# Token differences from raw tokens, unsplit in DRAM; four gate buffers; output weights split during the branch projections

## The chip, the core and the metric

The kernel runs on one core of one Trainium2 chip. The metric is the device time of one execution in microseconds, told as the median of several runs. The engines are TensorE (PE), VectorE (DVE), ScalarE (ACT), GpSimd (POOL) and SyncE (SP), whose queue issues most of the DMAs.

## The reference

One encoder block over 1024 tokens of width 1024, in float32. After an RMS norm, one input projection feeds three mixers and their gates, and a merge follows:

```python
h = rms_norm(x, g_pre)
a_qkv, bq, bk, bv, mq, ga, gb, gm, mg = split(h @ w_in)
oa = dilated_window_attention(rope(a_qkv), windows (128,1), (512,4), (2048,16)), merged by softmax of log-denominators
ob = grouped_query_attention(qk-norm, axial rope)          # 8 heads, 2 kv heads
om = cross_attention(mq, rms_norm(mem) @ w_mem_kv)         # 256 memory rows
ya, yb, ym = (oa * silu(ga)) @ w_br_a, (ob * silu(gb)) @ w_br_b, (om * silu(gm)) @ w_br_m
gates = sigmoid(mg + b_merge)                              # three times 1024 wide
merged = gates[0] * ya + gates[1] * yb + gates[2] * ym
out = x + rms_norm(merged @ w_out, g_post)
```

## The kernel before

**Split operands.** A float32 operand is held as two parts of a shorter format, a high part (a copy made by ACT) and a low part (the operand less the high part, made by DVE); the helper `split` issues these two. A product is then three matmuls: high by high, low by high, high by low. `hh[k]` and `hl[k]` are the two parts of the transposed tokens, scaled by `g_pre`, for the eight blocks of 128 channels; a tile is 128 x 1024.

**Stages, in order of time** (us from the start of the profiled span): start and memory branch (0 to 223), branch B with its attention (223 to 488), branch A (488 to 1050), the merge gates in pairs (1050 to 1272), the branch projections (1272 to 1413, called Y below), the output projection (1413 to the end). PE's order is written out by hand throughout: a weave interleaves attention pieces with dense units by their costs. In the pairs and in Y the orders of ACT, DVE, POOL and SP are the order of the code as well; in the branches a scheduler sets them, and `issue_after` holds a piece behind a named instruction.

**Gate pairs.** 22 of the 24 units of the gate projection are done two at a time, 11 pairs, by a Strassen-Winograd scheme with 7 products of half size in place of 8. A pair `n` runs through slots `i` = 0 to 6; in each, PE does one product of 12 matmuls (`prod`), DVE and ACT evacuate the product before (`evac`), and `slot` issues preparations: weight sums on POOL (`weight_sum`), their splits (`block_of`, `own_blocks`), weight loads (`load_pair`). The product order of all pairs but the last is A11, A12, S2, S3, S4, S1, A22, with the token operands B11, B21, T2, T3, B22, T1, T4. `gate_out` forms one gate half: an addition and a product on DVE into a buffer `rs`, then a tanh on ACT and a store to `thd` from ACT's queue. A pair stores four.

**Token differences.** T1 to T4 are differences of token blocks. They are made once, in branch B, by `token_block(k)` for four `k`: the sums `hh + hl` restore a block, DVE subtracts, `split` makes the two parts, and SP stores both to `tsd`. One of these steps is taken after a score maximum (`row_max`, L715) at positions 0, 1 and 3 of eight, as long as any are left. Before the last item of branch A, T2 and T3 are loaded (`load_block`); at the start of the pairs T1 and T4, between the weight loads of pair 1. T4 goes to `hh[0..3]` and `hl[0..3]`.

**Y.** 24 steps `m` (branch `n`, output block `f`), 24 matmuls each. In step `m`, after its matmuls are queued: evacuation of step `m - 1` (DVE multiplies by the gate `th`, POOL adds to `accs[f]`), loads for step `m + 2` (weights `wr`, gate `th` from `thd`), in some steps loads of a mixer output `ot` and its gate path `gt` and of `raw` reciprocals, their product and split into `hh`, `hl`, the weight split of step `m + 1`, and from step 15 on the loads of `w_out` into `raw`, split from step 16 on into `wo`.

**Output.** For each of eight token tiles, eight pieces of `accs` are split to an operand, then 48 matmuls, a norm, the residual and the store.

Of the kernel before, what the change touches and what calls it, by code (L numbers as in the profile page):

```python
# [14 lines left out]
D = 1024  # L15
# [35 lines left out]
def block(ctx: ExitStack, tc: tile.TileContext, x, xT, memT, cst, msk, bcst, tabA, gpost,  # L51
# [179 lines left out]
    wgd = dram.tile([4, 2, 3, S], F32, name="wgd")  # L231
    tsd = dram.tile([4, 4, P, 2, 512], F32, name="tsd")

# [410 lines left out]
    with tc.tile_pool(name="ba", bufs=1, reuse_waits="tile") as ba:  # L644
# [34 lines left out]
        def token_block(k):  # L679

            tb = [ba.tile([P, 512], F32, name=f"tb{j}", bufs=1) for j in range(4)]

            def whole(dst, i, e):
                return lambda: V.tensor_tensor(dst, hh[i][:, half[e]].bitcast(F32), hl[i][:, half[e]].bitcast(F32), op=OP.add)

            def sub(dst, x, y):
                return lambda: V.tensor_tensor(dst, x, y, op=OP.subtract)

            def store(j, src):
                def fn():  # L690
                    h = ba.tile([P, 512], R, name="tbh", bufs=2)
                    l = ba.tile([P, 512], R, name="tbl", bufs=2)
                    split(h, l, src)
                    for x, part in enumerate((h, l)):
                        nc.sync.dma_start(tsd[j, k, :, x], part.bitcast(F32))
                return fn

            b11, b12, b22, b21 = tb
            return [whole(b12, k, 1), whole(b11, k, 0), sub(b11, b12, b11), store(0, b11),
                    whole(b22, k + 4, 1), sub(b12, b22, b12), store(2, b12),  # L700
                    sub(b22, b22, b11), store(1, b22), whole(b21, k + 4, 0), sub(b21, b21, b22), store(3, b21)]

        def b_att():
# [69 lines left out]
            for n in range(128 + LAG_F + 8):  # L773
                if n < 128:
                    i, x = divmod(n, 8)
                    row_max(i, x)
                    if n % 32 == 0:
                        blocks += token_block(n // 32)
                    if blocks and x in (0, 1, 3):
                        with tc.issue_after(fp["last"].ins):  # L780
                            blocks.pop(0)()
                    yield 216
                    if i % 2 and i < 15 and x == 4:
                        q_prep((i + 1) // 2)
                        yield 436
                else:
                    yield END_PAD
                if n % 8 == LAG_S % 8 and 0 <= n - LAG_S < 128:
                    shift((n - LAG_S) // 8)
                    yield 109  # L790
                m = n - LAG_T
                if m < 0:
                    yield START_PAD
                elif m < 128:
                    scores(*divmod(m, 8))
                    yield 432
                m = n - LAG_P
                if 0 <= m < 128 and m % 8 == 7:
                    pv(m // 8)
                    yield 8 * 432  # L800
                m = n - LAG_F
                if m >= 0 and m % 8 == 7 and m < 128:
                    final(m // 8)
                    yield 432
# [27 lines left out]
    with tc.tile_pool(name="aa", bufs=1, reuse_waits="tile") as aa:  # L832
# [237 lines left out]
        def plan(it, pre, nxt):  # L1070
# [3 lines left out]
            def combining(T):  # L1074
                if todo and T == STEP_T[-len(todo)]:
                    with tc.issue_after(fp["last"].ins):
                        todo.pop(0)()

            def ready():
                if pre and pre["key"][1] == 2:  # L1080
# [4 lines left out]
            for T in range(NT if it else 4):  # L1085
# [4 lines left out]
                if it:  # L1090
                    out.append(it["soft"][T])
                out.append((lambda T=T: combining(T), 0.0))
                if T < 2:
                    if pre:
# [87 lines left out]

        TB, WHOLE = {}, {}

        def token_tiles(nm, tiles):
            for t in tiles:
                k = len(TB.setdefault(nm, []))
                WHOLE[nm, k] = t
                TB[nm].append([t[:, half[x]] for x in range(2)])

        def load_block(nm, ks=None):
            for k in ks or range(len(TB[nm])):
                src = tsd[int(nm[1]) - 1, k]
                if (nm, k) in WHOLE:
                    nc.sync.dma_start(WHOLE[nm, k].bitcast(F32), src.rearrange("p x t -> p (x t)"))
                else:
                    for x in range(2):
                        nc.sync.dma_start(TB[nm][k][x].bitcast(F32), src[:, x])

# [7 lines left out]
        for n in range(len(seq)):  # L1207
# [7 lines left out]
            if last:  # L1215
# [5 lines left out]
                load_block("T2")  # L1221
                load_block("T3")
            pieces = plan(items[n], items[n - 1] if n else None, items[n + 1])
            if last:
# [13 lines left out]
    SF = [sr.tile([P, 512], F32, name=f"sf{j}") for j in range(4)]  # L1238
    token_tiles("T1", [ab.tile([P, S], R, name=f"a{c}", bufs=2) for c in "qk"])
    token_tiles("T1", [t1l.tile([P, S], R, name=f"T1{k}") for k in (2, 3)])  # L1240
# [38 lines left out]
    def gate_out(n, u, t, x, z):  # L1279
        r = sr.tile([P, 512], F32, name="rs", bufs=2)  # L1280
        j = pairs[n][u]
# [27 lines left out]
    def g_load(i, k):  # L1309
        ot = pre["p"].tile([P, S], F32, name="ot", bufs=4)  # L1310
        nc.sync.dma_start(ot, od[i, k])
        gt = pre["p"].tile([P, S], F32, name="gt", bufs=2)
        nc.sync.dma_start(gt, g2d[i, k])
        GG[i, k] = [ot, gt]

    def r_load(k):
        rt = my.tile([P, S], F32, name="raw", bufs=2)
        for h in range(2):
# [32 lines left out]
    def slot(n, i):  # L1351
# [7 lines left out]
        for nm in todo_[i] if i < len(todo_) else ():  # L1359
            block_of(n, nm)  # L1360
        if n < last:
            if i == 3:
# [35 lines left out]
    load_pair(1, 0)  # L1398
    load_block("T1", (0, 1))
    load_pair(1, 1)  # L1400
    load_block("T1", (2, 3))
    load_block("T4")
    before = None
    for n in range(len(pairs)):
# [23 lines left out]
    def th_load(m):  # L1428
        if m < len(steps):
            _, i, f = steps[m]  # L1430
            THS[m] = my.tile([P, S], F32, name="th", bufs=3)
            nc.sync.dma_start(THS[m], thd[8 * i + f])

    def wo_load(k):
        raws[k] = my.tile([P, D], F32, name="raw", bufs=2)
        nc.sync.dma_start(raws[k], wout[k])
# [13 lines left out]
    def y_evac(m, s):  # L1450
# [6 lines left out]
        else:  # L1457
            V.scalar_tensor_tensor(th, th, 1.0, sv, op0=OP.add, op1=OP.mult)  # L1458
            G.tensor_tensor(accs[f], accs[f], th, op=OP.add)  # L1459

    th_load(0)
    th_load(1)
    yp = None
    for m, (n, i, f) in enumerate(steps):
# [14 lines left out]
        if n < 2:  # L1479
            if f - 1 in (0, 1, 3, 5):  # L1480
                g_mult(j, f // 2)
            if f - 2 in (0, 1, 3, 5):
                g_split(j, (f - 1) // 2, slice(0, S))
        if m >= 15 and m < 23:
            wo_load(m - 15)
        if n == 2:
            split(*wo[f], raws[f])
    y_evac(*yp)
    manual.__exit__(None, None, None)

# [5 lines left out]
    for T in range(NT):  # L1496
        t = slice(T * 128, T * 128 + 128)
        ah = wp.tile([P, 8, 128], R, name="wh")
        al = wp.tile([P, 8, 128], R, name="wl")
        for k in range(8):  # L1500
            A.activation(ah[:, k], accs[k][:, t], AF.Copy, scale=0.5)
            V.scalar_tensor_tensor(al[:, k], accs[k][:, t], 0.5, ah[:, k].bitcast(F32), op0=OP.mult, op1=OP.subtract)
        sv = pss().rearrange("p a b -> p (a b)")
# [163 lines left out]
```

## Time and profile before

| | |
|---|---|
| median of 3 runs | 1517.31 us (1515.16 to 1519.26) |
| the profiled execution's own time | 1514.58 us |
| its span in the profile | 1512.8 us |
| mean granted TensorE clock | 0.993 |
| busy share of the span: PE, DVE, ACT, POOL | 97%, 64%, 41%, 35% |
| DMA | 151.26 MB, mean 100 GB/s |

The page of the profile gives busy time per engine; the views of the trace give stretches, groups of instructions, and waits. A wait line names the waiting engine and line, and what ended the wait. Matmuls are pipelined: one is shown 0.39 us long while the next starts sooner, so a busy PE is not a PE at its pace. Each row of stretches has, per engine, busy time and the number of instructions.

### The profile page before, as it was taken

What the parts mean: (1) busy time and instruction counts of PE and PEld (TensorE: products, weight loads), DVE (VectorE), ACT (ScalarE), POOL (GpSimd) and SP (SyncE); (2) the same over time, 40 slices, a digit from 0 to 9 for tenths busy, and PEclk for the clock granted to TensorE, in tenths of its full rate; (3) what the DMA queues carried; (4) which work ended last, traced back from release to release, by engine and by line L of the source; (5) the groups of instructions that cost most, each with busy time, mean ns of one, the idle gap of its engine ahead of it and who ended that gap; (6) DMA issues with size and microseconds to landing.
All of it is one profiled execution on the core that took longest, in us unless ns stands there. A gap on an engine that the chain in (4) does not pass through costs nothing.

```text
span 1512.8 us, 20951 instructions
## 1 busy us (share of the span) xinstructions
PE 1463.6 (97%) x7712; PEld 1161.6 (77%) x7712; DVE 972.2 (64%) x1701; ACT 617.4 (41%) x1396; POOL 523.1 (35%) x401
## 2 busy tenths in 40 slices
PE   8999988999999999999999999999999999999998
PEld 7899965556556888888888888888788777787787
DVE  7755569888874566556656856653677677565543
ACT  6534444555555145344443444344333333122321
POOL 1426314656657232123223312311344221034422
PEclk9999999999999999999999999999999999999999
DMA  6322022122121210112112111343543444856332
GB/s 241 100 97 70 29 64 79 63 75 66 66 79 58 88 42 29 43 44 72 56 43 73 44 42 49 104 137 108 187 133 121 150 163 160 253 211 234 114 110 97
DMA packets 69014, 151.26 MB, mean 100 GB/s; under 512 B 15344, under 2 KB 25264, under 8 KB 68784
## 3 DMA queue, kind: packets, MB, share of 16 engines
q1 hardware_dynamic: 62432, 138.27, 27.6%
q10 hardware_dynamic: 6480, 11.67, 2.1%
q8 instruction: 60, 0.98, 0.3%
q14 instruction: 42, 0.34, 0.1%
HBM read 111.79 MB, written 38.11 MB: 99 GB/s over the span
## 4 chain that ended last, share of the span: by engine, by line
PE 64%; DVE 13%; issue 9%; DMA 5%; ACT 4%; POOL 4%; SPq 0%; ACTq 0%; DVEq 0%; POOLq 0%
PE d L143 12%; PE d L147 12%; PE d L145 12%; PE sc L1518 4%; PE s L125 4%; PE ov L748 3%; PE tr L1015 3%; PE s L952 2%; DVE bn L715 2%; DMA thd<-rs 2%; DMA raw<-in_wout 2%; PE d L534 2%; DVE og L1151 1%; DVE rs L1283 1%; PE s L733 1%
## 5 line engine op out<-in xcount | busy, mean ns | idle before, releaser
L143 PE MATMUL d<-hh,wh 128*128 128x512 f32 x864 | 346.0, 400 | 3.9 <-DVE fth L222 3.9
L147 PE MATMUL d<-hh,wl 128*128 128x512 f32 x864 | 347.0, 402 | 0.0
L145 PE MATMUL d<-hl,wh 128*128 128x512 f32 x864 | 342.4, 396 | 0.0
L143 PEld LDWEIGHTS d<-hh,wh 128*128 128x128 f32 x864 | 162.9, 189 | 45.3 <-issue 7.7
L147 PEld LDWEIGHTS d<-hh,wl 128*128 128x128 f32 x864 | 162.9, 188 | 36.0 <-issue 5.2
L145 PEld LDWEIGHTS d<-hl,wh 128*128 128x128 f32 x864 | 162.9, 189 | 34.8 <-issue 4.7
L105 ACT ACTIVATE wh<-wr 128x1024 fp32r<-128x1024 f32 (+1 forms) x89 | 83.6, 942 | 232.8 <-PE d L145 155.3
L739 POOL TENSOR_TENSOR bl<-bl,bp 128x512 f32<-128x512 f32 x96 | 137.7, 1435 | 67.7 <-ACT bp L735 62.4
L125 PE MATMUL sc<-hh,wh 128*128 128x512 f32 x384 | 120.9, 395 | 7.1 <-ACT wh L105 2.7
L871 POOL TENSOR_TENSOR aq<-t1a,t2a 128x512 f32<-128x512 f32 x24 | 54.6, 2274 | 163.5 <-DVE t1a L865 163.5
L865 DVE SCALAR_TENSOR_TENSOR t2a<-d,tab 32x512 f32<-32x512 f32 x96 | 65.9, 687 | 62.8 <-PE d L147 57.8
L106 DVE TENSOR_TENSOR wl<-wr,wh 128x1024 fp32r<-128x1024 f32 x65 | 87.4, 1346 | 29.1 <-ACT wh L105 29.1
L735 ACT ACTIVATE bp<-s 128x512 f32<-128x512 f32 x128 | 75.1, 594 | 50.8 <-PE s L733 50.0
L871 POOL TENSOR_TENSOR ak<-t1a,t2a 128x512 f32<-128x512 f32 x24 | 55.1, 2296 | 117.5 <-DVE t1a L864 117.5
L715 DVE TENSOR_REDUCE bn<-tr 128x1 f32<-128x512 f32 x128 | 85.6, 682 | 13.7 <-PE tr L714 13.0
L125 PEld LDWEIGHTS sc<-hh,wh 128*128 128x128 f32 x384 | 72.4, 190 | 25.5 <-DVE wh L106 4.6
L1459 POOL TENSOR_TENSOR acc<-acc,th 128x1024 f32<-128x1024 f32 x16 | 45.6, 2848 | 125.4 <-DVE th L1458 125.4
L1254 POOL TENSOR_TENSOR sf<-wr 128x512 f32<-128x512 f32 x22 | 28.8, 1331 | 154.0 <-DVE ch L106 101.2
L864 DVE TENSOR_TENSOR t2a<-d,tab 32x512 f32<-32x512 f32 x96 | 66.0, 687 | 24.9 <-PE d L147 21.2
L964 DVE CUSTOM_DVE_ANT_0 pra<-s,mask 128x192 f32<-128x192 f32 (+2 forms) x192 | 56.7, 348 | 33.9 <-PE s L952 23.8
L125 PE MATMUL sc<-hl,wh 128*128 128x512 f32 x192 | 75.6, 394 | 1.2 <-DVE hl L106 1.2
L1001 ACT ACTIVATE app<-tr 128x384 f32<-128x384 f32 (+2 forms) x96 | 45.9, 478 | 71.6 <-PE tr L998 46.2
(299 smaller groups left out, 3160.7 us busy)
## 6 DMA issues: line engine op xcount, KB each, us to landing
wr<-in_wu SPq DMA_DIRECT2D x76, 512.0 KB
th<-thd SPq DMA_DIRECT2D x24, 512.0 KB
thd<-rs ACTq DMA_DIRECT2D x44, 256.0 KB
g2d<-fth SPq DMA_DIRECT2D x24, 256.0 KB
wgt<-wgd SPq DMA_DIRECT2D x24, 256.0 KB
ot<-od SPq DMA_DIRECT2D x12, 512.0 KB
gt<-g2d SPq DMA_DIRECT2D x12, 512.0 KB
wr<-in_wbr SPq DMA_DIRECT2D x24, 256.0 KB
```

Of the source, the lines that this page charges most:

```text
L105: A.activation(dst_h, src, AF.Copy)
L106: V.tensor_tensor(dst_l, src, dst_h.bitcast(F32), op=OP.subtract)
L125: PE.matmul(out_ps, a, b, start=i == 0, stop=i == n - 1)
L143: PE.matmul(dst, wh[:, k, :], hh[k][:, t], start=k == 0, stop=False)
L145: PE.matmul(dst, wh[:, k, :], hl[k][:, t], start=False, stop=False)
L147: PE.matmul(dst, wl[:, k, :], hh[k][:, t], start=False, stop=k == 7)
L715: fp["last"] = V.tensor_reduce(st[i]["n"][:, j, c:c + 1], s, axis=AX.X, op=OP.min)
L735: A.activation(pp, s, AF.Exp, scale=-1.0)
L739: G.tensor_tensor(lsum[i % 2], lsum[i % 2], pp, op=OP.add)
L864: return V.tensor_tensor(out, x, y, op=OP.mult)
L865: return V.scalar_tensor_tensor(out, x, scale, y, op0=OP.mult, op1=OP.mult)
L871: G.tensor_tensor(half_of(o, half, g), classes(t1, g), classes(t2, g), op=OP.add)
```

## The change

Token differences are made from the raw tokens: `token_block` loads two tiles of `xT`, scales them by `g_pre` on ACT in place, subtracts on DVE and stores each difference once, unsplit. `tsd` is half as large. T2, T3 and the first half of T1 are loaded before or in the last item of branch A, the rest of T1 and T4 at the start of the pairs, all into the low tile; `split_block` splits in place on use: T2 and T3 in the last item of A, T1 and T4 in slots 2 to 5 of pair 0. `rs` gets four buffers, `th` four, `raw` three, `gt` one and, for some, a `raw` buffer. `w_out` is loaded in steps 10 to 17 and split in steps 12 to 19. The first output operand is split in step 23 and behind the last evacuation, and the last accumulation is done on DVE.

```diff
-    tsd = dram.tile([4, 4, P, 2, 512], F32, name="tsd")
+    tsd = dram.tile([4, 4, P, 512], F32, name="tsd")
...
         def token_block(k):
-            tb = [ba.tile([P, 512], F32, name=f"tb{j}", bufs=1) for j in range(4)]
-            def whole(dst, i, e):
-                return lambda: V.tensor_tensor(dst, hh[i][:, half[e]].bitcast(F32), hl[i][:, half[e]].bitcast(F32), op=OP.add)
-            def sub(dst, x, y):
-                return lambda: V.tensor_tensor(dst, x, y, op=OP.subtract)
-            def store(j, src):
+            x1, x2 = [ba.tile([P, S], F32, name=f"tx{j}", bufs=1) for j in range(2)]
+            for j, t in enumerate((x1, x2)):
+                nc.sync.dma_start(t, xT[k + 4 * j])
+                A.activation(t, t, AF.Copy, scale=cs[:, C_GP + k + 4 * j:C_GP + k + 4 * j + 1])
+            (b11, b12), (b21, b22) = [[t[:, h] for h in half] for t in (x1, x2)]
+            T = [ba.tile([P, 512], F32, name=f"tb{j}", bufs=1) for j in range(4)]
+            def sub(j, x, y):
                 def fn():
-                    h = ba.tile([P, 512], R, name="tbh", bufs=2)
-                    l = ba.tile([P, 512], R, name="tbl", bufs=2)
-                    split(h, l, src)
-                    for x, part in enumerate((h, l)):
-                        nc.sync.dma_start(tsd[j, k, :, x], part.bitcast(F32))
+                    V.tensor_tensor(T[j], x, y, op=OP.subtract)
+                    nc.sync.dma_start(tsd[j, k], T[j])
                 return fn
-            b11, b12, b22, b21 = tb
-            return [whole(b12, k, 1), whole(b11, k, 0), sub(b11, b12, b11), store(0, b11),
-                    whole(b22, k + 4, 1), sub(b12, b22, b12), store(2, b12),
-                    sub(b22, b22, b11), store(1, b22), whole(b21, k + 4, 0), sub(b21, b21, b22), store(3, b21)]
+            return [sub(0, b12, b11), sub(2, b22, b12), sub(1, b22, T[0]), sub(3, b21, T[1])]
...
-                    if n % 32 == 0:
-                        blocks += token_block(n // 32)
-                    if blocks and x in (0, 1, 3):
+                    if n in (18, 42, 66, 90):
+                        blocks += token_block((n - 18) // 24)
+                    if blocks and x in (1, 3) and n % 24 != 19:
...
+            def tokens(T):
+                if T >= 2:
+                    for nm, k in late[:2]:
+                        with tc.issue_after(fp["last"].ins):
+                            split_block(nm, k)
+                    del late[:2]
+                if T == 5:
+                    token_tiles("T1", [ab.tile([P, S], R, name=f"a{c}", bufs=2) for c in "qk"])
+                    load_block("T1", (0, 1))
...
+                if it and not nxt:
+                    out.append((lambda T=T: tokens(T), 0.0))
...
-        def load_block(nm, ks=None):
-            for k in ks or range(len(TB[nm])):
-                src = tsd[int(nm[1]) - 1, k]
-                if (nm, k) in WHOLE:
-                    nc.sync.dma_start(WHOLE[nm, k].bitcast(F32), src.rearrange("p x t -> p (x t)"))
-                else:
-                    for x in range(2):
-                        nc.sync.dma_start(TB[nm][k][x].bitcast(F32), src[:, x])
+        def load_block(nm, ks=range(4)):
+            for k in ks:
+                nc.sync.dma_start(TB[nm][k][1].bitcast(F32), tsd[int(nm[1]) - 1, k])
+        def split_block(nm, k):
+            h, l = TB[nm][k]
+            split(h, l, l.bitcast(F32))
+        late = []
...
+                late += [("T2", k) for k in range(4)] + [("T3", k) for k in range(4)]
...
-        r = sr.tile([P, 512], F32, name="rs", bufs=2)
+        r = sr.tile([P, 512], F32, name="rs", bufs=4)
...
-        gt = pre["p"].tile([P, S], F32, name="gt", bufs=2)
+        gt = my.tile([P, S], F32, name="raw", bufs=3) if i < 2 and k % 2 else pre["p"].tile([P, S], F32, name="gt", bufs=1)
...
-        rt = my.tile([P, S], F32, name="raw", bufs=2)
+        rt = my.tile([P, S], F32, name="raw", bufs=3)
...
+        if first:
+            for nm, k in {2: (("T1", 0), ("T1", 1)), 3: (("T1", 2), ("T1", 3)), 4: (("T4", 0), ("T4", 1)),
+                          5: (("T4", 2), ("T4", 3))}.get(i, ()):
+                split_block(nm, k)
...
     load_pair(1, 0)
-    load_block("T1", (0, 1))
-    load_pair(1, 1)
     load_block("T1", (2, 3))
     load_block("T4")
+    load_pair(1, 1)
...
-            THS[m] = my.tile([P, S], F32, name="th", bufs=3)
+            THS[m] = my.tile([P, S], F32, name="th", bufs=4)
...
-        raws[k] = my.tile([P, D], F32, name="raw", bufs=2)
+        raws[k] = my.tile([P, D], F32, name="raw", bufs=3)
...
-            G.tensor_tensor(accs[f], accs[f], th, op=OP.add)
+            (V if m == 23 else G).tensor_tensor(accs[f], accs[f], th, op=OP.add)
+    def out_split(ah, al, T, k):
+        src = accs[k][:, T * 128:T * 128 + 128]
+        A.activation(ah[:, k], src, AF.Copy, scale=0.5)
+        V.scalar_tensor_tensor(al[:, k], src, 0.5, ah[:, k].bitcast(F32), op0=OP.mult, op1=OP.subtract)
+    WO = (4, 5, 6, 7, 0, 1, 2, 3)
...
-        if m >= 15 and m < 23:
-            wo_load(m - 15)
-        if n == 2:
-            split(*wo[f], raws[f])
+        if m >= 10:
+            if m < 18:
+                wo_load(WO[m - 10])
+            if 12 <= m < 20:
+                split(*wo[WO[m - 12]], raws[WO[m - 12]])
+        if m == 23:
+            first = out_operand()
+            for k in range(6):
+                out_split(*first, 0, k)
     y_evac(*yp)
+    for k in (6, 7):
+        out_split(*first, 0, k)
```

## The prediction

> **What bounds the kernel now.** I read the stages first (busy time per stretch: PE, weight loads, DVE, ACT, POOL, then granted clock, DMA share, GB/s), then PE's waits.
>
> ```profile
> core 0: us, PE busy (x) PEld busy (x) DVE busy (x) ACT busy (x) POOL busy (x), PEclk, DMA share, GB/s
> 223.00:488.00 265.00, 252.84 (x1065) 157.94 (x1065) 208.44 (x292) 141.82 (x243) 155.69 (x110) 1.00 0.21 72
> 488.00:1049.90 561.90, 561.50 (x3337) 454.25 (x3335) 332.81 (x752) 227.63 (x680) 155.15 (x95) 1.00 0.20 61
> 1049.90:1271.90 222.00, 215.72 (x926) 174.59 (x924) 160.10 (x203) 84.28 (x128) 68.63 (x42) 0.98 0.46 153
> 1271.90:1413.00 141.10, 132.83 (x568) 107.16 (x569) 84.05 (x81) 32.56 (x43) 38.79 (x14) 0.99 0.68 232
> 1413.00:1512.80 99.80, 91.28 (x418) 75.85 (x416) 45.23 (x84) 23.52 (x85) 29.31 (x24) 0.97 0.25 90
> ```
> ```profile
> engine line waited for: us in total, times, longest us
> PE tr L714 <- DVE bn L715: 8.0, 20, 0.9
> PE s L371 <- ACT hh L272: 5.8, 1, 5.8
> PE tr L596 <- DVE pm L588: 4.2, 2, 2.6
> PE s L125 <- ACT ch L105: 4.1, 3, 2.4
> PE d L143 <- DVE fth L222: 3.9, 2, 2.2
> PE sc L125 <- ACT wh L105: 2.7, 2, 1.6
> PE sc L125 <- DVE wh L106: 2.6, 3, 1.2
> PE sc L1518 <- DVE wl L1502: 2.3, 1, 2.3
> PE sc L125 <- DVE sp L1277: 1.9, 1, 1.9
> PE s L125 <- DMA hh<-tsd: 1.3, 1, 1.3
> PE sc L125 <- DVE hl L106: 1.2, 1, 1.2
> ```
>
> The stretches shown are: branch B, branch A, the gate pairs, the branch projections ("Y"), the output projection. The 223 us before them hold the start and the memory branch, which the change leaves alone. PE is the bound in all of them, so an edit pays only where it removes a PE wait. Branch A has none (561.5 of 561.9 us). The change touches the other waits from B on: L714 and L143 (B), `ch` and `hh<-tsd` (pairs), `sp` (the join), the rows with `sc` (Y and output).
>
> Waits alone understate the loss. The pace of undisturbed matmuls is the distance of their starts:
>
> ```profile
> 1092.32 0.39 PE L125 MATMUL s<-hh,wh 128*128 128x512 f32 x1
> ...
> 1097.53 0.39 PE L125 MATMUL s<-hh,wl 128*128 128x512 f32 x1
> ```
>
> These are the first and last of 24: 5.21 / 23 = 0.2265 us. The pairs have 11 x 7 x 12 = 924 matmuls, 209.3 us at that pace, and took 222.0: 12.7 lost. Y has 24 x 24 = 576, 130.5 us, and took 141.1: 10.6 lost. What a short wait costs is seen around the one for `hh<-tsd`:
>
> ```profile
> 1070.30 0.67 PE L125 MATMUL s<-hl,ch 128*128 128x512 f32 x1 [0.30 <-DMA hl<-tsd]
> ```
> ```profile
> 1068.00:1070.00 2.00, 0.67 (x2) 0.19 (x1) 1.65 (x3) 1.00 (x2) 0.00 (x0) 1.00 0.90 275
> 1070.00:1072.00 2.00, 1.70 (x4) 1.00 (x5) 0.00 (x0) 1.07 (x2) 0.00 (x0) 0.62 1.07 255
> 1072.00:1074.00 2.00, 2.00 (x6) 1.56 (x6) 0.00 (x0) 0.00 (x0) 0.00 (x0) 0.53 0.73 279
> ```
>
> Twelve matmuls in 6 us instead of 26.5 is 3.3 us lost for 1.6 us of waiting (1.3 for `hh`, 0.3 for `hl`), because the granted clock fell to 0.53. The Trainium skill (TensorE: Matmul & The Clock Gate, Part 1: The HAM clock gate) states that the clock halves after an idle window of about 3.4 us; by that rule gaps of 1 to 2 us cost only themselves, and the sum below would be some 5 us smaller. The trace shows the halving after 1.6 us, so I keep the surcharge.
>
> **Branch B: token differences from raw tokens.**
>
> ```profile
> L684 DVE TENSOR_TENSOR tb<-hh,hl x16: 671/1170/1509, 225.2 to 456.0; 128x512 f32<-128x512 f32 x16
> L687 DVE TENSOR_TENSOR tb<-tb,tb x16: 670/1064/1781, 228.8 to 458.1; 128x512 f32<-128x512 f32 x16
> L105 ACT ACTIVATE tbh<-tb x16: 613/630/632, 229.5 to 459.3; 128x512 fp32r<-128x512 f32 x16
> L106 DVE TENSOR_TENSOR tbl<-tb,tbh x16: 678/1036/1806, 233.4 to 461.3; 128x512 fp32r<-128x512 f32 x16
> ```
> ```profile
> L105 ACT ACTIVATE wh<-wr 128x1024 fp32r<-128x1024 f32 x65 | 68.7, 1058 | 161.7 <-PE d L145 155.3 <-ACT rs L1284 3.6 <-DMA wr<-in_wu 1.4
> ```
> ```profile
> 255.37 0.50 PE L143 MATMUL d<-hh,wh 128*128 128x512 f32 x1 [2.17 <-DVE fth L222]
> ```
>
> Before: 48 DVE operations at medians of 1.17, 1.06 and 1.04 us, 52 us. After: the 16 subtractions, 17 us. DVE loses 35 of its 208 us. ACT drops 16 x 0.63 = 10.1 and gains 8 scalings of 128x1024 at 1.06 = 8.5. SP drops 32 stores of 256 KB and gains 8 loads of 512 KB and 16 stores: the same bytes in a stretch with DMA share 0.21, so nothing. L714's PE waits are for the row minima `bn`, which stand in DVE's queue behind these operations; the new code places them two steps apart instead of back to back. Two thirds of the operations go, so of the 8.0 us, plus 20 x 0.17 (a matmul is shown 0.39 long at a pace of 0.2265, which hides 0.17 of each gap), plus the L143 wait of 2.2, whose DVE row came late for the same reason, two thirds would be 9. I take **6**, since minima still queue behind other evacuations; bounds 2 and 10, and below nothing by a rival.
>
> **End of branch A.** Eight splits (ACT 0.63, DVE about 0.7 to 1.1 each: 5 and 6 to 9 us) come into its last item. DVE works 333 of 562 us there and ACT 228, and PE has dense work beside it: **0**. Without that cover it would be up to 9.
>
> **Pair 0.** The late transfers were the last of 5.1 MB queued at its start; now 2.5 MB stand there, unsplit, so `hh<-tsd` lands in time. In exchange eight more splits lie in slots 2 to 5, behind in-order work:
>
> ```profile
> 1063.57 0.63 ACT L105 ACTIVATE ch<-sf 128x512 fp32r<-128x512 f32 x1 [3.70 <-POOL sf L1254]
> ```
>
> That is pair 1's S3 block, waiting for POOL's weight sum. T4's first two splits stand behind it on ACT, the other two behind the S2 block after it. From 1063.6 I count ACT done with the last at about 1067 and DVE (S3, T4, T4, evacuation, S2, T4, T4 at 0.7 to 1.1) at about 1069.6. The product A22 starts at 1049.9 + 6 x 2.72 = 1066.2 and wants its third low part at 1067.8, ready at 1069: a wait of 1.2 with some surcharge, 2 to 3 instead of 3.3. I take **1**, bounds -3 and 3. The next late thing is POOL's sums. (`load_pair(1, 1)` moves behind T4's loads but still has under 2.5 MB ahead, against 2 MB before.)
>
> **Four gate buffers.**
>
> ```profile
> DVE rs L1277 <- DMA thd<-rs: 28.3, 11, 6.4
> ```
>
> Once per pair the third gate of the burst S1, S1, A22 waits for the first one's store, up to 6.4 us. Behind it stand on DVE all evacuations and splits, on ACT the tanh and the next `ch` split, for which PE then waits (the 2.4 in `ch` is this one). With four buffers no gate waits for a store of its own burst. Of the 12.7 us lost in the pairs, 3.3 are T4's; the other 9 are mostly these `ch` waits (4.1 plus surcharge) and pieces I can't name. I take **5**, bounds 3 and 7. At the join, the first Y product waits 1.9 for `sp`, the second 1.6 for ACT's `wh` behind the last tanh, both behind such a store; 3.5 and a surcharge of about one. I take **4**, bounds 1 and 5.
>
> **Y: th with four buffers, output weights earlier.**
>
> ```profile
> SPq L1432 <- POOL acc L1459: 60.4, 13, 7.2
> ```
> ```profile
> L1459 POOL TENSOR_TENSOR acc<-acc,th 128x1024 f32<-128x1024 f32 x16 | 45.6, 2848 | 125.4 <-DVE th L1458 125.4
> ```
> ```profile
> L106 DVE TENSOR_TENSOR wh<-wr,wh 128x512 fp32r<-128x512 f32 x24 | 16.4, 684 | 1.8 <-ACT wh L105 1.8
> L1458 DVE SCALAR_TENSOR_TENSOR th<-th,sc 128x1024 f32<-128x1024 f32 x16 | 19.4, 1213 | 2.8 <-PE sc L125 2.8
> ```
> ```profile
> 1345.55 3.42 DVE L106 TENSOR_TENSOR hl<-ot,hh 128x1024 fp32r<-128x1024 f32 x1
> ```
> ```profile
> L106 DVE TENSOR_TENSOR hl<-raw,hh x4: 1226/1226/2059, 1378.3 to 1394.4; 128x1024 fp32r<-128x1024 f32 x4
> ```
>
> SP's queue stands for `th` slots, and every later load with it; a fourth buffer lets each go one step (5.44 us) earlier. The waits `wh L106` (2.6) and `hl L106` (1.2) follow late loads, so with surcharge about 5 of the 10.6 lost in Y hang on this (the rest is the join). Against it: six weight loads (3 MB) move into steps 10 to 15, which makes 13 MB in 43.5 us for steps 8 to 15, 299 GB/s, where the stretch averaged 232 at share 0.68, so about 340 when full. It fits, narrowly. At steps 13 and 14 the weight load's slot is freed only by that same step's split, so SP, and the next `wr` and `th` behind it, stand some 3 us. DVE gains a split in steps 12 to 15: evacuation 1.2, `wh` 0.7, `hl` up to 3.4, weight split 1.2, 6.5 against 5.44 in two of four steps; the lag of 2 us is inside the 3.5 that the next `wh` has. I take **3.5**, bounds -2 and 6.
>
> **Output.** Six of eight first operand tiles move ahead of the last Y unit's end, and the last accumulation goes from POOL (2.8) to DVE (about 1.2). The wait of 2.3 for `wl L1502` with a surcharge of 1.5 goes. I take **3**, bounds 1 and 4.
>
> The Trainium skill (GPSIMD Engine Reference, Specifications) says that DVE instructions with two SBUF inputs contend with GpSimd; the rows 3.42 against 1.23 agree, and by it the moved splits are the last rival here.
>
> **Sum**: 6 + 0 + 1 + 5 + 4 + 3.5 + 3 = 22.5. The profiled execution took 1514.6 (its span 1512.8 and 1.8 around it), so 1492 for such a one; the median of the three runs lies 2.7 higher, 1517.3, so **1495**. The terms' bounds give 7 to 35 off.
>
> **Rivals.**
> *Half comes back.* B's minima queue behind other DVE work and pair 0's splits make PE wait as long as the transfers did: B 2, pair 0 -2, the join 2, Y 1, the rest as above: 11 off, 1506. For it: DVE is 72% busy in the pairs (160.1 of 222). Against: 28 us of that stretch was DVE waiting.
>
> *Slower: ACT behind the raw tokens.* The eight scalings wait in ACT's strict order for their loads. A 512 KB load took
>
> ```profile
> 1383.95 5.10 DMA raw<-in_wout
> ```
>
> and PE has two score banks at about 1.9 us a score (128 in the 238 us to the last `tbl` at 461.3), so ACT may stand some 2.5 us before PE stands. Where a scaling sits right behind its load's issue, PE stops 2.6 us, with the surcharge (3.3 for 1.6) 5.4. Eight of these are 43 us at most, 21 without surcharge; with B's 6 gone, 16.5 remain off and 21 to 43 come on: 1522 to 1544, say 1523. It decides once loads land over 2.5 us after the scaling's turn. Against: the load is issued seven score steps ahead of the first subtraction, and ACT has 123 us free in B.
>
> *Contention in Y.* Weight splits fall beside POOL's sum and take 3.42 like `hl`: steps 12 to 15 then hold 30.6 us of DVE against 21.8, a lag of 8.8 less 3.5, so PE loses 5 and a surcharge of 2, and Y's 3.5 go: 1506. Against: the sum covers 2.8 of each 5.44 us, so rarely two splits.
>
> **How the numbers follow.** Forecast 0.58, half back 0.18, contention 0.09, slower 0.15. A measurement tells 0.3% (4.6 us) from no change. Slower takes that rival's 0.15 less 0.02 for a mild form: 0.13; that and the low ends of the two 1506 cases give 0.07 for the same; faster 0.80. The predicted time is the forecast's own. The range goes from 1484 (terms near their good bounds) to 1515 (the bad bounds and part of the slower case).
>
> **What would show it.** In the profile after: L714's waits under 4 us; no `rs <- thd<-rs` wait; no `hh<-tsd` wait but perhaps one for T4's split; the `sp` and `L1502` waits gone; SP's `th` wait far under 60. Wrong would be ACT waits for `tx` loads in B with PE's score matmuls behind them, or new PE waits for `hl`, `wh` in steps 12 to 17.

## The result, and the profile after

The median of four runs after the change is 1484.65 us (1480.33 to 1485.02), against 1518.28 us (1515.16 to 1520.06) for the kernel before beside it: a ratio of 0.9774, 95% interval 0.9749 to 0.9799. The kernel is faster by 33.6 us. The prediction said 1495, so its sign held and its size was 11 us short; by the ratio (0.9774 x 1517.31 = 1483.0) the time lies 1 us below the low end of its range. The profiled execution took 1480.33 us, its span 1478.5.

The busy time per stretch of the kernel after, cut at the same events as before (branch B, branch A, pairs, Y, output):

```profile
core 0: us, PE busy (x) PEld busy (x) DVE busy (x) ACT busy (x) POOL busy (x), PEclk, DMA share, GB/s
223.00:471.90 248.90, 245.85 (x1061) 159.58 (x1061) 172.83 (x260) 141.71 (x235) 148.59 (x110) 1.00 0.23 76
471.90:1034.30 562.40, 561.82 (x3338) 454.60 (x3337) 337.75 (x760) 232.04 (x688) 155.38 (x95) 1.00 0.20 58
1034.30:1245.40 211.10, 209.85 (x928) 173.47 (x925) 170.11 (x215) 89.44 (x138) 68.71 (x42) 1.00 0.44 146
1245.40:1384.50 139.10, 133.30 (x577) 108.68 (x576) 103.78 (x84) 33.16 (x48) 41.15 (x15) 0.99 0.73 242
1384.50:1478.50 94.00, 87.78 (x410) 73.50 (x409) 40.16 (x76) 21.06 (x77) 22.49 (x22) 0.98 0.26 90
```

Most of the gain lies in two stretches, B and the pairs. To compare kernels I cut each trace at PE events (first row-maximum matmul of B, start of B's last block of 16 value products, first A score, first pair product, first Y product, first output product). In the two profiled executions this gives, in us:

| | B | A | pairs and join | Y | output |
|---|---|---|---|---|---|
| before | 263.78 | 517.21 | 223.80 | 141.16 | 97.92 |
| after | 248.27 | 517.53 | 211.12 | 139.29 | 93.73 |
| gain | 15.5 | -0.3 | 12.7 | 1.9 | 4.2 |

With 0.4 in the start these sum to 34.3 us of span. The 44.9 us between B's last block of value products and A's first score did not change.

The waits of PE after, the groups that answer to those shown of before:

```profile
PE sc L125 <- DVE wh L106: 3.4, 2, 2.2
PE sc L125 <- ACT wh L105: 2.2, 2, 1.9
PE d L143 <- DVE fth L222: 1.7, 1, 1.7
PE tr L707 <- DVE bn L708: 1.3, 3, 0.5
...
PE s L125 <- DVE hl L106: 1.3, 1, 1.3
```

L707 is before's L714: its 20 waits for a row minimum (`row_max` takes it of negated scores) have become 3. The waits for `ch`, for `sp`, for the transfers from `tsd` and for the output's first low part have no row any more. What is left of the pairs is a single wait, for a split of T4 in pair 0, and 5.6 us of the waits from B on lie in Y, in the two `sc` rows. DVE's row of waits for the store of a gate (28.3 us before) is gone as well.

### The profile page after: what moved, and what is told of

Its sections match the earlier page's. It is cut to its first block, busy times and chain, and to the rows that moved or that the text cites. A ratio compares the mean times of both kernels' runs of the same rounds, so it can differ in the third digit from the quotient of the medians.

```text
span 1478.5 us, 20900 instructions
## 1 busy us (share of the span) xinstructions
PE 1446.5 (98%) x7712; PEld 1160.2 (78%) x7712; DVE 966.6 (65%) x1686; ACT 625.3 (42%) x1404; POOL 511.8 (35%) x400
## 3 DMA queue, kind: packets, MB, share of 16 engines
q1 hardware_dynamic: 60272, 134.07, 28.3%
## 4 chain that ended last, share of the span: by engine, by line
PE 83%; DVE 6%; ACT 3%; POOL 2%; DMA 2%; issue 2%; SPq 0%; POOLq 0%; DVEq 0%; ACTq 0%
PE s L125 14%; PE d L143 12%; PE d L147 12%; PE d L145 12%; PE sc L125 8%; PE sc L1538 5%; PE ov L741 3%; PE tr L1008 3%; PE s L945 2%; PE d L534 2%; PE s L726 1%; PE s L725 1%; PE tr L707 1%; DMA th<-thd 1%; PE tr L991 1%
## 5 line engine op out<-in xcount | busy, mean ns | idle before, releaser
L143 PE MATMUL d<-hh,wh 128*128 128x512 f32 x864 | 345.8, 400 | 1.9 <-DVE fth L222 1.7
L143 PEld LDWEIGHTS d<-hh,wh 128*128 128x128 f32 x864 | 162.9, 189 | 43.4 <-issue 7.7
L732 POOL TENSOR_TENSOR bl<-bl,bp 128x512 f32<-128x512 f32 x96 | 130.8, 1362 | 60.8 <-ACT bp L728 55.3
L1465 POOL TENSOR_TENSOR acc<-acc,th 128x1024 f32<-128x1024 f32 x15 | 41.2, 2743 | 120.5 <-DVE th L1464 120.5
L965 ACT ACTIVATE pra<-pra,sts 128x128 f32<-128x128 f32 (+2 forms) x152 | 66.5, 439 | 20.0 <-DVE sts L957 20.0
```

Of the source, the lines that this page charges most:

```text
L143: PE.matmul(dst, wh[:, k, :], hh[k][:, t], start=k == 0, stop=False)
L732: G.tensor_tensor(lsum[i % 2], lsum[i % 2], pp, op=OP.add)
L965: A.activation(src, raw, AF.Exp, scale=-1.0, bias=bias, accum_out=sts[:, h, 1, T:T + 1])
```

## The experiments

"B" below is the first column of the table; each kernel differs from the one after by the edit shown, unless it is said to start from the one before.

### Branch B: how many operations, and where

Theory: DVE's queue ahead of the row minima is the cost, through the number of operations. Rival: their places decide.

```diff
+                    V.tensor_tensor(T[j], x, y, op=OP.subtract)
+                    V.tensor_tensor(T[j], x, y, op=OP.subtract)
                     V.tensor_tensor(T[j], x, y, op=OP.subtract)
```

> The changed kernel with each token subtraction in branch B done three times (48 DVE operations as before, in the 16 places of the change; the result is the same). Theory N (the number of DVE operations ahead of the row minima cost the 15.5 us in B): B, from its first row maximum to its last value product, goes back from 248 to about 260 us or more, the time to about 1497. Theory P (the place: back to back at positions 0 and 1, the burst at B's start, DVE standing for ACT's high part): B stays within 248 to 252, the time within 3 us of 1484.

The median was 1498.12 us (1493.73 to 1500.27), ratio to before 0.9865 (0.9838 to 0.9892). B took 265.09, all of its gain given back. The run is not clean, though: its waits of PE and, in B, of ACT show two causes.

```profile
PE s L727 <- ACT bp L730: 7.0, 5, 2.3
...
PE tr L709 <- DVE bn L710: 4.9, 9, 1.1
```
```profile
ACT tx L684 <- DMA tx<-in_xT: 12.9, 6, 4.5
```

The waits for the minima came back in part, but ACT also stood 12.9 us for raw tokens (4.5 of them at the first load, much as after), and PE 7.0 us for ACT's exponentials. The two belong together: each of these five PE waits ends 1.7 to 1.8 us after the start of a scaling that stood for its load. The first pair, from the timelines of ACT and PE:

```profile
291.47 1.15 ACT L684 ACTIVATE tx<-tx,cs 128x1024 f32<-128x1024 f32 x1 [1.37 <-DMA tx<-in_xT]
```
```profile
293.16 0.50 PE L727 MATMUL s<-QH,KS 128*128 128x512 f32 x1 [2.27 <-ACT bp L730]
```

That is the mechanism of the "slower" rival, at work once the scaling's turn comes 1.4 to 1.8 us ahead of its data. To leave it out, the same 48 operations were given places of their own (`again` is the subtraction without its store):

```diff
-            return [sub(0, b12, b11), sub(2, b22, b12), sub(1, b22, T[0]), sub(3, b21, T[1])]
+            out = []
+            for j, x, y in ((0, b12, b11), (2, b22, b12), (1, b22, T[0]), (3, b21, T[1])):
+                out += [again(j, x, y), again(j, x, y), sub(j, x, y)]
+            return out
...
-                    if blocks and x in (1, 3) and n % 24 != 19:
+                    if blocks and x in (1, 3, 4, 5, 6, 7) and not 19 <= n % 24:
```

> The changed kernel with three subtractions in place of each one in branch B, as before 48, but each in a place of its own (positions 1, 3, 4, 5, 6, 7 of eight). Theory N (number): B at 258 us or more, PE waits for the row maxima 6 us or more. Theory P (bursts: three in a row, or two back to back): B at 253 or less. Theory A (the last kernel with 48 lost time to ACT standing for raw token loads, 12.9 us, not to DVE): B long only if ACT again waits over 8 us for them.

One run, 1489.38 us; B took 257.71, 9.4 more than after and just under theory N's 258. The same stretch, of the spread kernel and then of the one after, and PE's waits of the spread kernel for the minima:

```profile
225.00:475.00 250.00, 240.78 (x1030) 152.79 (x1030) 204.48 (x289) 135.84 (x225) 147.66 (x106) 1.00 0.23 74
```
```profile
225.00:475.00 250.00, 247.63 (x1071) 159.60 (x1071) 171.00 (x255) 140.25 (x231) 151.53 (x112) 1.00 0.23 76
```
```profile
PE tr L721 <- DVE bn L714: 6.5, 6, 2.0
PE tr L713 <- DVE bn L714: 1.9, 5, 0.5
```

The second of these waits is that of the row maxima: 1.9 us, where theory N asked for 6. The first, L721, belongs to another product, the transposition of an item's gathered minima in `shift`, which had no wait before (its line there is L722):

```profile
L722 PE MATMUL tr<-cs,bnm 128*68 128x128 f32 x16 | 4.3, 271 | 0.0
```

Summed over the distances of matmul starts, 7.7 of the 9.4 us arose at these 16 products and 1.2 at the 128 row maxima, where the kernel before had its loss. So 33.5 us more of DVE work cost 9.4 us, 0.3 per operation, but the run does not separate number from place: its operations at positions 3 to 7 are one step apart too, and they moved PE's wait to another product.

Next the opposite: the 16 operations stay and their places move together.

```diff
-                    if blocks and x in (1, 3) and n % 24 != 19:
+                    if blocks and x in (1, 2) and n % 24 != 18:
```

> The changed kernel with its 16 subtractions at positions 1 and 2 of eight, one score step apart, in place of 1 and 3. Theory P: the back to back places cost, B goes from 248.3 to 251 or more, the PE waits for the row maxima from 1.3 to 3 or more. Theory N: B within 0.7 us of 248.3.

One run, 1483.7 us. B took 252.15: 3.9 us more for neighbouring places alone, as theory P has it. PE's wait for the minima went from 1.3 to 2.9.

```profile
PE tr L707 <- DVE bn L708: 2.9, 5, 0.9
```

Last, on the kernel before, the differences from raw tokens with the split and the two stores of before: 32 DVE operations (16 differences, 16 low parts), one at each of the old places 0, 1 and 3. A block's loads start at the row maxima where the change has them.

```diff
-            return [whole(b12, k, 1), whole(b11, k, 0), sub(b11, b12, b11), store(0, b11), ...
+            return [sub(b11, b12, b11), store(0, b11), sub(b12, b22, b12), store(2, b12),
+                    sub(b22, b22, b11), store(1, b22), sub(b21, b21, b22), store(3, b21)]
```

> The kernel before with the differences made from raw tokens but still split and stored as two parts in branch B: 32 DVE operations, 16 of them behind ACT, at positions 0, 1 and 3. Number and place both count by now (48 in places of their own cost 9.4 us more than 16, 16 put one step apart cost 3.9 more). Theory N (number mostly, some 0.3 us for each operation): from the first row maximum to the first score of branch A 300 to 304 us, between 308.7 (48) and 293.2 (16). Theory P (place mostly, since positions 0 and 1 stay): 305 or more.

One run, 1505.29 us; B took 256.32, a gain of 7.5 over before with the 16 sums gone; the 16 low parts, with the other places, make the 8.1 that are left. To A's first score it is 301.2, in theory N's range. PE's wait for the minima stood between the two kernels:

```profile
PE tr L713 <- DVE bn L714: 3.7, 10, 0.8
```

Both theories hold in part. B in order of DVE operations: 48 as before 263.8, 48 spread 257.7, 32 at the old places 256.3, 16 close together 252.2, 16 as in the change 248.3. In each of these kernels PE stands for DVE's queue. How the 15.5 us divide between number and place the runs do not settle: place alone is worth 3.9 us with 16 operations, 48 differ by 6.1 between the old places and the spread ones (where ACT's halves of the splits and the second stores are gone too), and 16 operations fewer at the old places are worth 7.5.

### The pairs: gate buffers against T4's late splits

```diff
-        r = sr.tile([P, 512], F32, name="rs", bufs=4)
+        r = sr.tile([P, 512], F32, name="rs", bufs=2)
```

> The changed kernel with two gate buffers again. Theory G (the gate buffers carry nearly all that the pairs and the join gained): the stretch from the first pair product to the first Y product goes from 211 to 220 to 222 us, the time to about 1494. Rival T (the token transfers carry it): 211 goes to at most 215, the time to at most 1488.

1497.74 us, ratio 0.9863 (0.9837 to 0.9889). Pairs and join took 226.84, 15.7 more than after, 3.0 more than before, and more than theory G's 220 to 222. The waits of PE for the splits of `ch` are back:

```profile
PE s L125 <- ACT ch L105: 5.7, 4, 2.8
...
PE s L125 <- DVE ch L106: 2.4, 2, 2.1
```

And the other way round, four buffers in the kernel before (`raw` and `gt` arranged as after, to have the space):

```diff
-        r = sr.tile([P, 512], F32, name="rs", bufs=2)
+        r = sr.tile([P, 512], F32, name="rs", bufs=4)
```

> The kernel before with four gate buffers, and with gt and raw arranged as in the change so that they fit. Theory G: the stretch from the first pair product to the first Y product goes from 224 to about 214 us, with the wait for the late T4 transfer (3 to 4 us) still there; the time 1507 to 1509. Rival T: 218 or more.

1505.48 us, ratio 0.9919 (0.9894 to 0.9945). Pairs and join took 212.30: the buffers, with the arrangement they need, bring 11.5 of the 12.7 us, and no `ch` row is left. For the transfers of T4, which the change unsplits, 3 to 4 us of waiting were expected; PE waits only this, and 0.4 for `hh`:

```profile
PE s L125 <- DMA hl<-tsd: 1.0, 2, 0.7
```

Unsplit transfers with the splits on use are thus worth 1.2 us beside four buffers (212.30 to 211.12), and cost 3.0 beside two (223.80 to 226.84), each from one profiled execution.

### Y: the fourth gate tile, and the order of SP's queue

```diff
-            THS[m] = my.tile([P, S], F32, name="th", bufs=4)
+            THS[m] = my.tile([P, S], F32, name="th", bufs=3)
```

> The changed kernel with three th buffers. If the fourth buffer is what lets the loads of Y's steps 8 to 16 come in time, as forecast: the PE waits for hl and wh near step 16 (2.2 us before) come back and Y goes from 139.3 to 142 or more. If it does nothing there: Y within 0.7 us of 139.3.

One run, 1486.89 us; Y took 145.08, 5.8 more than after and more than in any other run. Its waits of PE:

```profile
PE sc L125 <- DVE wh L106: 5.1, 5, 2.2
...
PE sc L125 <- ACT wh L105: 2.5, 2, 1.4
```

The waits that before had 96 to 100 us into Y are back (1.42 at 1344.33 and 1.53 at 1346.59), so the fourth tile works as forecast, as far as one run shows. Not all of the 5.8 need be its own: the granted clock over Y was 0.96 in this run and 0.99 after. Yet Y gained only 1.9 in the profiled executions. One of SP's waits around Y's start in the kernel after, then its timeline there, show what came in place of the old waits:

```profile
SPq L1438 <- DMA thd<-rs: 10.0, 1, 10.0
```
```profile
1240.23 10.79 SPq L1438 DMA_DIRECT2D th<-thd  x2
1251.13 0.37 SPq L1342 DMA_DIRECT2D wr<-in_wbr  x1
```

The second `th` load waits until the last gate's store is done, and every later load of Y waits behind it. The stretches (columns as in the table of stretches) show DMA idle, then full, and PE stopped:

```profile
1244.00:1248.00 4.00, 4.00 (x20) 3.30 (x19) 3.10 (x6) 0.72 (x1) 0.00 (x0) 1.00 0.00 1
...
1264.00:1266.00 2.00, 0.89 (x3) 0.46 (x4) 1.69 (x2) 1.04 (x1) 0.00 (x0) 1.00 1.05 418
1270.00:1272.00 2.00, 1.74 (x7) 0.82 (x5) 1.88 (x2) 1.25 (x2) 0.00 (x0) 1.00 1.05 410
1272.00:1274.00 2.00, 0.02 (x1) 0.00 (x0) 2.00 (x3) 1.07 (x2) 0.00 (x0) 1.00 1.01 401
1274.00:1276.00 2.00, 1.73 (x4) 1.45 (x5) 2.00 (x3) 0.00 (x0) 0.00 (x0) 0.50 1.07 365
1276.00:1278.00 2.00, 2.00 (x7) 1.52 (x7) 1.93 (x3) 0.00 (x0) 0.00 (x0) 0.64 1.01 214
```

The stand is also there with two gate buffers, and with three `th` tiles it falls on a later load, of `raw`; the two rows are of those kernels:

```profile
SPq L1438 <- DMA thd<-rs: 12.4, 1, 12.4
```
```profile
SPq L1322 <- DMA thd<-rs: 7.1, 1, 7.1
```

Before, SP stood 5.0 and 3.9 us for a gate's store, at its loads of `gt` and `raw`. So the stand is not new; its place goes with the fourth `th` tile and not with the gate buffers. That the second `th` tile lies on space which the gate buffers held until then is my reading of the releaser; it was not tried by itself. What was tried is to put loads that need not stand ahead of the one that does:

```diff
     th_load(0)
+    y_load(2)
+    g_load(1, 0)
     th_load(1)
...
-        y_load(m + 2)
+        if m:
+            y_load(m + 2)
...
```

> The changed kernel with the loads of y weights 2, ot and gt of the first product moved ahead of the second th load, at which SP stands 10 us for the last gate store. Theory Q (that stand in SP's queue makes the PE waits in Y's units 3 to 5): these waits (5.6 us) fall under 2, Y goes from 139 to 134 or 135 us, the time to about 1480. Rival W (the DMA engines are full there, share 1.0 from 1256 to 1288, so order does not matter): Y stays at 138 to 139.5, the time at 1484.

1477.93 us (1476.73 to 1479.59), ratio 0.9736 (0.9714 to 0.9759). The weights, the mixer output and its gate path now go out while SP would stand:

```profile
1242.17 0.37 SPq L1342 DMA_DIRECT2D wr<-in_wbr  x1
1243.79 0.33 SPq L1314 DMA_DIRECT2D ot<-od  x1
1244.17 0.42 SPq L1316 DMA_DIRECT2D gt<-g2d  x1
1252.54 0.79 SPq L1438 DMA_DIRECT2D th<-thd  x2
```

Y took 136.56, between what the two theories said. PE's first wait there fell from 1.94 to 0.66 us; the second did not (2.25 after, 2.30 here), and together they are not under 2. So the second is not shown to come from SP's stand: it ends with a weight split on DVE, behind products that waited for `raw` loads at a DMA share of 1.0, and what would shorten it was not tried.

One profiled Y proves little by itself: in the kernels whose edits lie in B alone, Y's code being the same, it took 135.42 to 137.84 against 139.29 after, so that the change's gain in Y is 1.9 to 5.7 us by these executions. The four times, all below the lowest of the four after, say more, though they were not run beside those, and the two intervals overlap.

### Output: operand early, weights early

```diff
-        if m == 23:
-            first = out_operand()
-            for k in range(6):
-                out_split(*first, 0, k)
```

(and the last accumulation back on POOL)

> The changed kernel with the first output operand split only after the last evacuation and the last accumulation on POOL, as before; the early load and split of the output weights stays. If the early operand split carries the 4.2 us gained at the output: that stage goes from 93.7 to 97 or 98 us with a wait of 2 to 3 us for the low part. If the earlier weight split carries it (DVE and ACT free at the end): at most 95.

One run, 1480.0 us; the output took 93.72. Then the other half, the operand early and the weights as before:

```diff
-        if m >= 10:
-            if m < 18:
-                wo_load(WO[m - 10])
-            if 12 <= m < 20:
-                split(*wo[WO[m - 12]], raws[WO[m - 12]])
+        if m >= 15 and m < 23:
+            wo_load(m - 15)
+        if n == 2:
+            split(*wo[f], raws[f])
```

> The changed kernel with the output weights loaded and split in the steps of the kernel before (15 to 22 and 16 to 23); the first operand is still split early. The reverse (late operand, early weights) kept the output stage at 93.7. If the early weight split carries the 4.2 us: 97 or more. If each alone is enough: 95 or less, and then it is the sum of work at the seam, of which either half can stay. Y, freed of 3 MB of loads in steps 10 to 15: within 1.5 us of the changed kernel's if they cost nothing there.

One run, 1485.13 us; the output took 93.80. Either half alone brings the output to 93.7 or 93.8; together they bring no more. In neither kernel does PE wait in the output stage. The 4.2 us themselves vary with the execution: the two runs made on the kernel before, with its output code, took 98.3 and 95.4 there. Y took 142.33 here, with a wait of 3.9 for `wh` 20 us after its start, ahead of step 10 where the moved loads begin, so I don't put its length down to the edit.

### Both kernels beaten?

The order of loads from above, and all four splits of T4 in slot 4:

```diff
-            for nm, k in {2: (("T1", 0), ("T1", 1)), 3: (("T1", 2), ("T1", 3)), 4: (("T4", 0), ("T4", 1)),
-                          5: (("T4", 2), ("T4", 3))}.get(i, ()):
+            for nm, k in {2: (("T1", 0), ("T1", 1)), 3: (("T1", 2), ("T1", 3)), 4: (("T4", 0), ("T4", 1),
+                          ("T4", 2), ("T4", 3))}.get(i, ()):
...
+    y_load(2)
+    g_load(1, 0)
     th_load(0)
...
```

> The changed kernel with three loads of Y (weights 2, ot and gt of the first product) ahead of both first th loads, and with all four T4 splits in slot 4 of pair 0, ahead of the split that waits for POOL's weight sum. If SP's stand at the th slots and the T4 split behind pair 1's block are what is left: the first wait of PE in Y's units 3 to 5 falls under 2 us and Y to 134 or 135 us (136.6 with the loads between the two th loads), the wait of 1.3 for hl in pair 0 goes and the pairs fall from 211.1 to 209.6; the time about 1475. If the DMA engines bound Y's beginning: Y stays at 136.5 or more, the time 1477 to 1478.

1476.02 us, median of five (1475.52 to 1478.95), ratio 0.9736 (0.9714 to 0.9757): faster than before by 40.6 us beside it. Pairs and join took 210.40, Y 134.30, the shortest of all runs. The waits of PE left there (the first is still over the 2 us that were expected, and the granted clock stayed at 1.00 behind it):

```profile
PE sc L125 <- DVE wh L106: 2.2, 1, 2.2
...
PE s L125 <- DVE hl L106: 0.5, 1, 0.5
```

All its times lie below those of the kernel after; as the two were not run beside each other and the intervals of their ratios overlap, the 0.4% between them is likely, not settled.

## Why the prediction had the sign and missed the size

**Branch B, 6 forecast, 15.5 measured.** This is the step that failed. Its inputs held: DVE was to lose 35 us and lost 35.6 (208.44 to 172.83), and ACT kept its load (141.82 to 141.71). What failed is the inference that with two thirds of the operations two thirds of the waits go, and the step down from 9 to 6 after it. The 13.6 us of loss that the prediction counted there (8.0, 3.4 hidden, 2.2) went nearly whole: summed over the distances of starts, the row maxima lost 9.5 us between the two kernels and the L143 product 3.1, together 12.6. In the rows, `bn` lost 6.7 of 8.0 us and the L143 wait of 2.2 all of it, and PE's idle time in B fell from 12.2 to 3.05. Taking 6 "since minima still queue behind other evacuations" was the second error in the same step: all that is left of that wait is 1.3. The remaining 2.9 us went at products that the sum did not count, the scores (1.7) above all. The upper bound of 10 fell with the step, as it was built from the same waits.

The price of a wait was also set too low. A late product of the kernel before, with its neighbours:

```profile
244.62 0.39 PE L143 MATMUL d<-hh,wh 128*128 128x512 f32 x1
245.90 0.50 PE L714 MATMUL tr<-KS,QH 128*128 128x512 f32 x1 [0.89 <-DVE bn L715]
246.24 0.39 PE L732 MATMUL s<-QH,KS 128*128 128x512 f32 x1
```

The two distances of starts are 1.28 and 0.34 us where the pace in B is 0.23, so 1.16 us are lost for 0.89 shown. The prediction counted the 0.17 ahead of the late product and not the 0.11 behind it. B's 26 waits of 12.1 us became 8 of 3.2; with 0.27 more for each of the 18 that went, this is 13.8 of the 15.5 us.

**End of branch A, 0 forecast, -0.3 measured.** Right; the dense work covers the splits.

**Pair 0, 1 forecast, 1.2 measured** (beside four buffers). The forecast wait of 1.2 is there, on the product that was named:

```profile
1053.82 0.50 PE L125 MATMUL s<-hl,ch 128*128 128x512 f32 x1 [1.25 <-DVE hl L106]
```

It comes 19.5 us after the pairs' start, where the prediction had 19.1. One detail was off: in the code T4's first two splits stand ahead of the S3 block and the last two between it and the S2 block, where the prediction had them behind these blocks. With all four in slot 4 the wait was 0.5.

**Four gate buffers, 5 and 4 at the join forecast, 11.5 to 15.7 measured.** The mechanism was right, the size was not. The term was set low for "pieces I can't name"; most of them were the same thing. In the run with two buffers 8.1 us of `ch` waits cost 15.7 us, a factor of 1.9, about the one that the prediction had read itself around the `hh` wait (3.3 for 1.6) and then did not use: before, 4.1 of `ch` and 3.5 at the join at that factor are 14. What the factor is made of is said at the end.

**Y, 3.5 forecast, 1.9 measured.** By the other executions of the same Y code it is up to 5.7, so this term is not shown to be wrong. The waits that the fourth tile removes came back without it, and SP's waits for POOL's sum fell from 60.4 to this:

```profile
SPq L1438 <- POOL acc L1465: 18.2, 10, 1.9
```

What the prediction did not see is the wait that the fourth tile moved to the head of SP's queue at Y's start, 10 us, with PE waits of 1.94 and 2.25 at 1263.9 and 1274.3 after it, of which moving the loads took away most of the first. The crowding that it feared instead, in steps 12 to 17, costs nothing there.

**Output, 3 forecast, 4.2 measured.** Near, with the cause too narrow: it was put down to the early operand and the faster accumulation, and the early weights alone do as much.

**The bounds.** The bounds of the terms add up to 2 and 35, not 7 and 35. Their good ends would have given 1482 us; the range was begun at 1484. B's 15.5 lay outside its own bounds all the same.

**The rivals.** "Half comes back" did not come: B and the buffers gave more, not less. "ACT behind the raw tokens" is there in a small way, at B's start, without any PE wait behind it:

```profile
ACT tx L684 <- DMA tx<-in_xT: 5.1, 3, 4.4
```

The run with every subtraction tripled shows the mechanism whole, with ACT 1.4 to 1.8 us late in place of the 2.5 that the prediction asked for; in the kernel after, the largest of these waits past the first load is 0.5. "Contention in Y" came with the size it was given, and met slack. DVE's splits in Y's second half, shortest, median and longest in ns:

```profile
L106 DVE TENSOR_TENSOR hl<-ot,hh x4: 1214/3414/3420, 1313.3 to 1339.9; 128x1024 fp32r<-128x1024 f32 x4
L106 DVE TENSOR_TENSOR wol<-raw,woh x4: 1211/1212/1215, 1324.6 to 1343.2; 128x1024 fp32r<-128x1024 f32 x4
L106 DVE TENSOR_TENSOR hl<-raw,hh x4: 3410/3420/3422, 1346.1 to 1361.3; 128x1024 fp32r<-128x1024 f32 x4
```

Four of the eight weight splits, those beside POOL's sum, took 3.42 us in place of 1.21, one in each of steps 16 to 19, and PE waited 0.2 in all: these steps hold no operand split. In steps 10 to 15 three of the operand's four splits (`ot`) fell beside the sum, and the weight splits stayed at 1.21.

## What to carry to other kernels

Price short waits from the stretch: its length less its matmuls at their undisturbed pace is what can be won. The rows of waits show only part of it; here each wait cost some 0.27 us beyond its row, and some of the longer ones about 1.7 more through the granted clock. An engine's in-order queue ahead of a small operation that PE needs is worth clearing, and worth spacing, even when that engine is far from full. A buffer added to a pool moves the others; look again at which load then stands first in its queue, and put those that need not stand ahead of it.

## What the runs showed of the hardware

The granted clock fell to 0.50 in the 2 us behind a wait of 2.25 us (the row of 1274 to 1276 above), as it had fallen to 0.53 behind 1.6 us before. It was 0.64 in the next 2 us and 1.00 after that: some 3.4 us at half rate, a loss of 1.7. Not every such wait brought it down. Behind the 1.94 us at 1263.9 it stayed at 1.00 (the row of 1264 to 1266), and so it did behind 2.2 us in the last kernel; what decides is not shown. The Trainium skill (TensorE: Matmul & The Clock Gate, Part 1: The HAM clock gate) ties the half rate to an idle window of about 3.4 us; these rows have it after shorter waits.

The factor of 1.9 in the pairs comes out of the two prices. In the run with two gate buffers the clock fell three times there (0.51 in the 2 us from 1111, 0.52 from 1169, 0.50 from 1234), behind waits of 2.09, 2.78 and 1.71 us. The six waits for `ch` are 8.1 us, 0.27 more for each 1.6, and three falls 5.1: 14.8 of the 15.7 us. In B the granted clock was 1.00 throughout, and only the first price was paid.

Sixteen DVE operations of about 1 us, moved one score step closer together, cost 3.9 us of PE time with the DVE 70% busy (172.83 of 248.90 in the kernel after).
